# Modulation steps of the first layer, and the place of its rotations on the vector engine

## The chip, the cores and the metric

The kernel runs on one core of a Trainium2 chip, as one program. The metric is the device time of one execution in microseconds (us), the median of the runs. The core has a matrix engine (TensorE, PE), a vector engine (VectorE, DVE), a scalar engine (ScalarE, ACT), a general engine (GpSimd, POOL) and a queue that issues the transfers (SyncE, SP). Each engine works through its own instructions in its own order, and they wait for each other by semaphores.

## What is computed

The program holds a block of two layers (attention with a feed-forward part, retention with a feed-forward part) and two more hybrid layers behind it, for 256 positions of width 1024. The change touches the first layer of the first block, where half of the 16 heads are stick-breaking heads and half are block-attention heads whose q and k are rotated; with 256 positions and blocks of 256, these see only their own block, a causal softmax.

```python
def ada_mod(c, w, b):
    m = jax.nn.silu(c) @ w + b
    return jnp.split(m[:, None, :], 6, axis=-1)

def attn_hybrid_mixer(h, w_qkv, w_o, pos):
    B, S, _ = h.shape
    qkv = (h @ w_qkv).reshape(B, S, 3, N_ATT_HEADS, HEAD_DIM).transpose(2, 0, 3, 1, 4)
    q, k, v = qkv[0], qkv[1], qkv[2]
    sb = stick_breaking_attention(q[:, :N_SB_HEADS], k[:, :N_SB_HEADS], v[:, :N_SB_HEADS])
    qm = rotary(q[:, N_SB_HEADS:], pos)
    km = rotary(k[:, N_SB_HEADS:], pos)
    mb = moba_attention(qm, km, v[:, N_SB_HEADS:])
    o = jnp.concatenate([sb, mb], axis=1).transpose(0, 2, 1, 3).reshape(B, S, ATT_W)
    return o @ w_o

def first_block(...):
    for layer in range(DEPTH):
        shift_m, scale_m, gate_m, shift_f, scale_f, gate_f = ada_mod(c, ada_w[layer], ada_b[layer])
        h = modulate(rms_norm(x, norm_gains[layer, 0]), shift_m, scale_m)
        ...
        x = x + gate_m * y
        h = modulate(rms_norm(x, norm_gains[layer, 1]), shift_f, scale_f)
        x = x + gate_f * swiglu(h, ffn_w_gate_up[layer], ffn_w_down[layer])
```

## The kernel before

All products are made from pairs of rounded parts: a weight piece of 1 MB comes as `raw` (L326, SP queue), ACT casts it to `whi` (L346), DVE subtracts to get `wlo` (L347), two of each for one `raw`, and PE does three matmuls for one (L278). `raw` has three buffers in all, two for any load and one that takes every third.

The first layer's attention is in `layer0`. The projection to q, k and v of the stick-breaking heads is done in the start-up. `layer0` then makes three modulation jobs (L822; the gate, then shift and scale of the feed-forward part). `gemm_col` computes q and k of the rotated heads, two tiles of 128 rows each; as each is done, its `epi` (L850) rotates it on DVE (`rotary`, L611 to L614, from PSUM with the table `rope` into `rows`), PE transposes it (L282, `p<-ident,rows`), and ACT copies the result to `qT` or `kT` (L857). Between these matmuls stand the stick-breaking heads (`score`, `sb_job`: ACT L658 to L660 make `sbe`, DVE L661 and L663 make `sbs`, PE multiplies `sbs` by triangles, ACT L668 and DVE L669 make `aT`), their products with v (`av`, `p<-aT,v`, whose result is split into `oTq` on ACT and `oTk` on DVE, L486 and L487), then the rotated heads (`causal_job`, L627 to L637, tiles `sm` and `aT`), their products with v, and the output projection `w_ao` (`gemm_k`), behind which `res_norm` adds the residual (L549, L550) and makes the next norm (L512 to L524).

A modulation job (`ada_steps`, L559) is a matrix-vector product done on DVE. It has four steps. A step is one call of `feed` (L373): a load of 1 MB of `ada_w` into a `raw` buffer and two instructions L570, each of which adds one row block, scaled by one element of c, to `acc`. When four steps are done, `acc` is split (`acch` on ACT, L486; `accl` on DVE, L487) and two pairs of matmuls with ones sum it over the partitions into `bc` (L586, L588). Three jobs are twelve steps, 24 instructions L570. `pump` (L332) calls `feed`: for each weight load that it emits it adds `self.rate` to a credit, and one step is emitted for each whole unit of credit.

What sets the order: PE runs in program order, which a planner makes: jobs are generators that yield due times, and each matmul advances the planner's clock `now` by its modelled time. DVE, ACT, POOL and SP run in the order that the tile scheduler gives them by priority. An instruction has, in general, the priority of its place in the program; `self.first()` (L532) lifts those within it by `PRI` = 250.

Of the kernel before, what the change touches and what calls it, by code (L numbers as in the profile page):

```python
# [27 lines left out]
VLAG = 3  # L28
START = 'a0 w0 a1 a2 w1 a3 v0 a4 w2 a5 v1 a6 w3 a7'.split()
T_AO, T_DN, T_RO, T_OUT, T_O = 4, 7, 7, 8, 8  # L30
R_L0, R_FFN, R_L1 = 2.04, 0.65, 0.59
PRI = 250
D_EV0, D_ROT0, D_SOFT, D_SB = 5.11, 5.49, 11.39, 9.42
D_ADA0, D_ADAF, D_ADA1, D_FFN, D_FFN1 = 12.84, 50.82, 20.9, 11.5, 11.36
# [28 lines left out]
def chunks_of(K, blocks):  # L63
    out, off = [], 0
    kt = K // 128
    for cols in blocks:
        n, lst = len(cols), []
        step = max(1, 2048 // n)
        step = min(step, 4)
        for k0 in range(0, kt, step):  # L70
            nk = min(step, kt - k0)
            lst.append((off, k0, nk, n))
            off += 128 * nk * n
        out.append(lst)
    return out
# [169 lines left out]
class Kern:  # L245
# [569 lines left out]
    def layer0(self, lp):  # L815
        nc, V, A = self.nc, self.V, self.A
        with self.pool("l0") as p:
            self.ph, self.smb = p, 3
            hT, ps0 = self.startup(lp)
            self.tc.keep_in_program_order(A.preload_act_table_set("natural_log_exp_and_others"))  # L820
            self.rate = R_L0
            jobs = [self.ada(lp, 0, v) for v in (2, 3, 4)]  # L822
            rope = p.tile([128, 2, 3, 32], F32, name="rope64")
            nc.sync.dma_start(rope, self.a["k_rope64"].rearrange("p (t j d) -> p t j d", t=2, j=3))
            self.causal = p.tile([128, 384], F32, name="causal0")
            nc.sync.dma_start(self.causal, self.a["k_causal"])
            self.strict = p.tile([128, 2, 128], F32, name="strict")
            nc.sync.dma_start(self.strict, self.a["k_strict"].rearrange("p (j n) -> p j n", j=2))
            h = lambda k, t: (hT[t][0][:, k], hT[t][1][:, k])
            qT = [p.tile([128, 4, 256], F32, tag=f"q{j}", name=f"qT{j}") for j in range(2)]  # L830
            kT = [p.tile([128, 4, 256], F32, tag=f"k{j}", name=f"kT{j}") for j in range(2)]
            v = [p.tile([128, 2, 512], F32, tag=f"v{j}", name=f"v{j}") for j in range(2)]
            oT, aTs, sj, avj = [None, None], {}, {}, {}

            def qk0(t, w):
                rows = self.wk.tile([128, 512], F32, tag="rows", bufs=4, name=self.nm("rows"))
                A.copy(rows, ps0[t][w])
                yield D_EV0
                src = self.trs(rows, 4)
                d = (kT if w else qT)[0][:, :, t * 128:t * 128 + 128]  # L840
                if w:
                    A.copy(d, src)
                else:
                    A.activation(d, src, AF.Copy, scale=0.125)

            j0 = [self.spawn(qk0(t, w)) for t in range(2) for w in range(2)]
            for t in range(2):
                A.copy(v[0][:, t], ps0[t][2])

            def epi(b, t, _, ps):  # L850
                if b == 3:
                    A.copy(v[1][:, t], ps)
                    return
                rows = self.wk.tile([128, 512], F32, tag="rows", bufs=4, name=self.nm("rows"))
                self.rotary(rows, ps, rope, t, 8, 32)
                yield D_ROT0
                A.copy((qT if b == 1 else kT)[1][:, :, t * 128:t * 128 + 128], self.trs(rows, 4))  # L857

            def score(hd, deps):
                j, r = hd // 8, hd % 8  # L860
                pr, o = r // 2, (r % 2) * 64
                while not all(d.done for d in deps):
                    yield 0.7
                aTs[hd] = aT = p.tile([128, 3, 128], F32, tag="aT", bufs=AT0, name=self.nm("aT"))
                q, k = (lambda: qT[j][o:o + 64, pr]), (lambda: kT[j][o:o + 64, pr])
                yield from self.sb_job(q, k, aT) if j == 0 else self.causal_job(q, k, 0.125, aT)

            def av(pr, deps):
                j, r = pr // 4, pr % 4
                while not all(d.done for d in deps):  # L870
                    yield 0.7
                yield 1.5
                if oT[j] is None:
                    oT[j] = [p.tile([128, 4, 256], F32R, tag=f"{x}{j}", name=f"oT{x}{j}") for x in "qk"]
                pv = self.av_pair(v[j], 2 * r, [aTs.pop(2 * pr), aTs.pop(2 * pr + 1)])
                self.split(oT[j][0][:, r], oT[j][1][:, r], pv)

            ch = chunks_of(D, QKV_BLOCKS)
            for hd in range(8):
                sj[hd] = self.spawn(score(hd, j0), 1.0 + hd * SP_SB)  # L880
            for pr in range(4):

                avj[pr] = self.spawn(av(pr, [sj[i] for i in range(8)]), 1.0)
            qkj = self.gemm_col(h, "w_qkv", ch[1:3], epi, 1)
            for hd in range(8, 16):
                sj[hd] = self.spawn(score(hd, qkj), 0.5 + (hd - 8) * SP_MB)
            vj = self.gemm_col(h, "w_qkv", ch[3:4], epi, 3)
            for pr in range(4, 8):
                avj[pr] = self.spawn(av(pr, vj + [sj[i] for i in range(8, 16)]), 1.0)
            gate, = self.finish(jobs[0])  # L890

            def ho(k, t):
                self.wait(avj[k])
                return tuple(x[:, k % 4, t * 128:t * 128 + 128] for x in oT[k // 4])

            nxt = self.res_norm(gate, lambda: self.finish(jobs[1], jobs[2])[::-1])
            self.gemm_k(ho, "w_ao", 8, nxt.epi, tail=T_AO)
        return nxt
# [615 lines left out]
```

## Time and profile before

| | before |
|---|---|
| median of 3 runs | 1489.71 us (1488.64 to 1490.63) |
| profiled execution | 1490.03 us, span 1488.2 us |
| PE busy | 1453.1 us, 98% of the span |
| DVE busy | 1046.9 us, 70% |
| ACT busy | 814.3 us, 55% |
| mean granted clock of PE | 0.995 |

The profile is of one execution. The span runs from the first to the last instruction; the run's time has 1.8 us more around it. A line of a timeline gives the start in us, the duration, the engine, the line of the code, the operation, what it writes and reads, and, in brackets, how long the engine stood idle before it and for whom. Neighbouring rows of the same kind are put together (x16), and then the duration is that of the group. The modelled end of a matmul lies later than the start of the one behind it, so the distance of the starts is what one costs. The granted clock of PE is given as a share of its full speed.

### The profile page before, as it was taken

To read this page: it belongs to the slowest core of one execution; us is meant where nothing else is said; L and a number is where in the kernel's file an instruction comes from. 1 tells how busy PE (TensorE), PEld (TensorE's weight loads), DVE (VectorE), ACT (ScalarE), POOL (GpSimd) and SP (SyncE) were. 2 spreads that over 40 slices of the span, in tenths; PEclk is the share of its full clock that TensorE was granted. 3 is DMA by queue.
4 is the path that set the end of the run, shared out by engine and by line. 5 is a ranking of instruction groups with operands and counts; after the bars stand their busy time and mean duration, and the time that the engine had idled before them with its cause. 6 is when DMAs were issued, how large, how long until landed. Compare 5 with 4: busy or idle time off the path is not lost.

```text
span 1488.2 us, 20261 instructions
## 1 busy us (share of the span) xinstructions
PE 1453.1 (98%) x7724; PEld 1218.9 (82%) x7724; DVE 1046.9 (70%) x1677; ACT 814.3 (55%) x1369; POOL 96.8 (7%) x84
## 2 busy tenths in 40 slices
PE   7999999999999999999999999999999999999998
PEld 4776788887877888888878899988888879998887
DVE  4688898956988848866378656666666865556664
ACT  4657566643444535665266745566445664566551
POOL 0000000000000000000012011110001101111000
PEclk9999999999999999999999999999999999999999
DMA  9747587754776637745445355554645545555552
GB/s 379 275 175 278 186 327 291 285 210 180 278 277 232 257 139 266 272 170 207 150 144 198 128 183 179 178 200 166 212 140 205 170 142 188 164 173 198 184 176 79
DMA packets 52965, 306.67 MB, mean 206 GB/s; under 512 B 7546, under 2 KB 10490, under 8 KB 24580
## 3 DMA queue, kind: packets, MB, share of 16 engines
q1 hardware_dynamic: 52148, 305.14, 57.4%
q8 instruction: 61, 1.00, 0.3%
q10 hardware_dynamic: 720, 0.24, 0.1%
q14 instruction: 36, 0.29, 0.1%
HBM read 301.16 MB, written 1.05 MB: 203 GB/s over the span
## 4 chain that ended last, share of the span: by engine, by line
PE 76%; DVE 11%; ACT 4%; DMA 3%; POOL 3%; issue 2%; POOLq 0%; SPq 0%; DVEq 0%; ACTq 0%
PE p L278 73%; DVE wlo L347 5%; PE p L282 3%; DMA raw<-in_w_in_dram 3%; POOL dss L482 2%; ACT whi L346 1%; ACT dsm L1434 1%; DVE dsm L1432 1%; DVE dss L1379 1%; POOL qss L482 1%; ACT dsm L1436 1%; POOL ss L514 0%; DVE junk L522 0%; DVE rows L1381 0%; DVE res L549 0%
## 5 line engine op out<-in xcount | busy, mean ns | idle before, releaser
L278 PE MATMUL p<-whi,hT 128*128 128x512 f32 (+2 forms) x2432 | 763.7, 382 | 6.3 <-DVE hT L487 2.2
L347 DVE TENSOR_TENSOR wlo<-raw,whi 128x1024 fp32r<-128x1024 f32 (+2 forms) x474 | 538.3, 1161 | 149.3 <-ACT whi L346 146.0
L346 ACT CAST whi<-raw 128x1024 fp32r<-128x1024 f32 (+2 forms) x474 | 462.6, 1001 | 262.9 <-PE p L278 174.6
L278 PEld LDWEIGHTS p<-whi,hT 128*128 128x128 f32 x2432 | 453.1, 188 | 80.4 <-issue 8.3
L278 PE MATMUL p<-wlo,hT 128*128 128x512 f32 (+2 forms) x1216 | 453.0, 373 | 0.0
L278 PEld LDWEIGHTS p<-wlo,hT 128*128 128x128 f32 x1216 | 229.6, 189 | 30.3 <-issue 1.7
L278 PE MATMUL p<-hT,whi 128*128 128x512 f32 x576 | 199.2, 398 | 0.0
L278 PE MATMUL p<-hT,wlo 128*128 128x256 f32 x576 | 149.9, 281 | 0.0
L278 PEld LDWEIGHTS p<-hT,whi 128*128 128x128 f32 x576 | 103.8, 188 | 19.6
L278 PEld LDWEIGHTS p<-hT,wlo 128*128 128x128 f32 x576 | 108.7, 189 | 6.6
L570 DVE SCALAR_TENSOR_TENSOR acc<-raw,csc,acc 128x1024 f32<-128x1024 f32 x80 | 102.2, 1278 | 3.1 <-DMA raw<-in_ada_w_dram 2.8
L278 PE MATMUL p<-whi,al 128*128 128x512 f32 x176 | 69.5, 395 | 0.0
L278 PE MATMUL p<-wlo,ah 128*128 128x512 f32 x176 | 69.5, 395 | 0.0
L278 PE MATMUL p<-whi,ah 128*128 128x512 f32 x176 | 69.5, 395 | 0.0
L482 POOL TENSOR_TENSOR dss<-dss,mh 128x6 f32<-128x6 f32 x32 | 46.1, 1442 | 330.5 <-DVE dss L481 330.5
L1381 DVE TENSOR_TENSOR rows<-p,dss 128x384 f32<-128x384 f32 x32 | 17.8, 558 | 46.3 <-POOL dss L482 46.3
L954 ACT COPY fT<-p 128x256 f32<-128x256 f32 x72 | 25.8, 369 | 37.1 <-PE p L278 34.5
L1434 ACT ACTIVATE dsm<-dsm,dst 128x512 f32<-128x512 f32 x32 | 22.9, 716 | 41.0 <-DVE dst L1433 41.0
L514 POOL TENSOR_TENSOR ss<-ss,mh 128x1 f32<-128x1 f32 x14 | 13.4, 959 | 474.1 <-DVE ss L513 474.1
L278 PE MATMUL p<-whi,s 128*128 128x512 f32 x128 | 41.3, 397 | 0.0
L278 PEld LDWEIGHTS p<-whi,al 128*128 128x128 f32 x176 | 33.0, 187 | 8.1
L278 PEld LDWEIGHTS p<-wlo,ah 128*128 128x128 f32 x176 | 33.0, 187 | 8.0
(259 smaller groups left out, 1618.9 us busy)
## 6 DMA issues: line engine op xcount, KB each, us to landing
raw<-in_w_in_dram SPq DMA_DIRECT2D x48, 1024.0 KB, 4.9
raw<-in_w_gu_dram SPq DMA_DIRECT2D x44, 1024.0 KB, 5.6
raw<-in_ada_w_dram SPq DMA_DIRECT2D x40, 1024.0 KB, 5.0
raw<-in_w_in_dram SPq DMA_DIRECT2D x48, 768.0 KB, 4.4
raw<-in_w_ret_dram SPq DMA_DIRECT2D x24, 1024.0 KB, 4.9
raw<-in_w_dn_dram SPq DMA_DIRECT2D x22, 1024.0 KB, 5.0
raw<-in_w_qkv_dram SPq DMA_DIRECT2D x11, 1024.0 KB, 5.4
as<-in_ada_s_dram SPq DMA_DIRECT2D x16, 512.0 KB, 8.0
```

Source lines behind the costliest of these rows:

```text
L278: self.T.matmul(out, lhsT=lhsT, rhs=rhs, start=first, stop=last, skip_group_check=skip)
L282: self.T.transpose(out, in_, self.ident)
L346: for ins in (self.A.copy(hi[:, :m * n], src), self.V.tensor_tensor(lo[:, :m * n], src, hi[:, :m * n].bitcast(F32), ALU.subtract)):
L347: self.V.tensor_tensor(lo[:, :m * n], src, hi[:, :m * n].bitcast(F32), ALU.subtract)):
L482: self.G.tensor_tensor(ss, ss, self.mh[:, :n], ALU.pow)
L570: self.V.scalar_tensor_tensor(acc, r[:, j * D:j * D + D], self.sc[:, k:k + 1], acc, ALU.mult, ALU.add)
L954: A.copy(f, ps[:, 256:512])
L1379: V.tensor_reduce(ss[:, :6], sq[:, :384].rearrange("p (h d) -> p h d", d=64), AX.X, ALU.add)
L1381: V.tensor_tensor(rows[:, :384].rearrange("p (h d) -> p h d", d=64), ps.rearrange("p (h d) -> p h d", d=64), ss[:, :6, None].to_broadcast( ...
L1432: V.tensor_tensor_reduce(sm, ps[j], tabs[j][:, t * 128:t * 128 + 512], 1.0, NEG, ALU.add, ALU.max, st[:, 0:1])
L1434: A.activation(sm, sm, AF.Exp, bias=st[:, 2:3], scale=0.125, accum_out=st[:, 3:4])
L1436: A.activation(sm, sm, AF.Copy, scale=st[:, 3:4])
```

## The change

The rate at which modulation steps follow weight loads in the first layer goes from 2.04 to 1.36. Four steps, all of the first job, are emitted ahead of the loads of the three small tables (`rope`, `causal`, `strict`). And the rotation in `epi` stands within `self.first()`. In the changed file lines behind L822 are two lines further down, and those behind the rotation three.

```diff
-R_L0, R_FFN, R_L1 = 2.04, 0.65, 0.59
+R_L0, R_FFN, R_L1 = 1.36, 0.65, 0.59
...
             jobs = [self.ada(lp, 0, v) for v in (2, 3, 4)]
+            for _ in range(4):
+                self.feed()
             rope = p.tile([128, 2, 3, 32], F32, name="rope64")
...
                 rows = self.wk.tile([128, 512], F32, tag="rows", bufs=4, name=self.nm("rows"))
-                self.rotary(rows, ps, rope, t, 8, 32)
+                with self.first():
+                    self.rotary(rows, ps, rope, t, 8, 32)
                 yield D_ROT0
```

How this orders the engines, at three places. First DVE, where the first rotated tile (`rows_739` before, `rows_759` after) is made, directly behind the weight subtractions of the fourth projection load. Before:

```order
L611 TENSOR_TENSOR rows_739<-p_646,rope_624 128x512
L612 TENSOR_TENSOR rt_740<-p_646,rope_624 128x8x32
L613 TENSOR_TENSOR rt_740<-p_646,rope_624 128x8x32
L614 TENSOR_TENSOR rows_739<-rows_739,rt_740 128x512
L570 SCALAR_TENSOR_TENSOR acc_779<-raw_783,csc,acc_779 128x1024
L661 SCALAR_TENSOR_TENSOR sbs_700<-p_696,sbe_699 128x384
L570 SCALAR_TENSOR_TENSOR acc_779<-raw_783,csc,acc_779 128x1024
```

And after, the same place on DVE, where `acc_624` is the first job's sum:

```order
L570 SCALAR_TENSOR_TENSOR acc_624<-raw_632,csc,acc_624 128x1024 x2
L661 SCALAR_TENSOR_TENSOR sbs_720<-p_716,sbe_719 128x384
L570 SCALAR_TENSOR_TENSOR acc_624<-raw_636,csc,acc_624 128x1024
L661 SCALAR_TENSOR_TENSOR sbs_731<-p_727,sbe_730 128x384
L570 SCALAR_TENSOR_TENSOR acc_624<-raw_636,csc,acc_624 128x1024
L661 SCALAR_TENSOR_TENSOR sbs_742<-p_738,sbe_741 128x384
L570 SCALAR_TENSOR_TENSOR acc_624<-raw_640,csc,acc_624 128x1024
L611 TENSOR_TENSOR rows_759<-p_666,rope_644 128x512
L612 TENSOR_TENSOR rt_760<-p_666,rope_644 128x8x32
L613 TENSOR_TENSOR rt_760<-p_666,rope_644 128x8x32
L570 SCALAR_TENSOR_TENSOR acc_624<-raw_640,csc,acc_624 128x1024
L614 TENSOR_TENSOR rows_759<-rows_759,rt_760 128x512
```

The rotation's four instructions now stand behind the first job's steps and three L661, and within the last step; before, they stood ahead of all of these.

On ACT, the copy of that tile's transposes to `qT`. Before:

```order
L660 ACTIVATE sbe_759<-sbe_759 128x384
L659 ACTIVATE sbe_801<-sbe_801 128x384
L857 COPY qT_631<-p_811 128x4x128
L660 ACTIVATE sbe_801<-sbe_801 128x384
L668 ACTIVATE aT_695<-p_696 128x384
```

And after, on ACT at the same place (`acch_799` is the high part of the first job's sum, `raw_789` the next projection load):

```order
L660 ACTIVATE sbe_821<-sbe_821 128x384
L486 CAST acch_799<-acc_624 128x1024
L346 CAST whi_791<-raw_789 128x1024
L346 CAST whi_795<-raw_789 128x1024
L860 COPY qT_651<-p_831 128x4x128
L668 ACTIVATE aT_715<-p_716 128x384
```

The copy now stands behind the split of the first job's sum and behind two weight casts.

The third place is the second half of the output projection, on ACT, with the four casts `oTq` of the rotated heads' results (`raw_1335` and `raw_1421` before are the first two loads of the feed-forward part's weights, `raw_1343` and `raw_1391` after). Before:

```order
L486 CAST acch_1358<-acc_1205 128x1024
L486 CAST oTq_1382<-p_1384 128x256
L346 CAST whi_1337<-raw_1335 128x1024
L346 CAST whi_1341<-raw_1335 128x1024
L486 CAST oTq_1382<-p_1391 128x256
L486 CAST oTq_1382<-p_1398 128x256
L486 CAST oTq_1382<-p_1405 128x256
L346 CAST whi_1423<-raw_1421 128x1024
L346 CAST whi_1427<-raw_1421 128x1024
```

And after, on ACT:

```order
L346 CAST whi_1345<-raw_1343 128x1024
L346 CAST whi_1349<-raw_1343 128x1024
L486 CAST acch_1353<-acc_1024 128x1024
L637 COPY aT_1256<-p_1380 128x384
L346 CAST whi_1393<-raw_1391 128x1024
L346 CAST whi_1397<-raw_1391 128x1024
L486 CAST oTq_1401<-p_1403 128x256
L486 CAST oTq_1401<-p_1413 128x256
L486 CAST oTq_1401<-p_1420 128x256
```

All four `oTq` now stand behind the casts of the second load of the feed-forward part, whose first cast moved ahead of them from behind them. On DVE `oTk` moved in the same way behind `wlo_1394` and `wlo_1398`, and on PE three matmuls of the projection now follow the first product with v, where before all four products came first.

## Rows read from the trace of the kernel before

**Rows 1.** The page's part 4: the chain that ended last, by engine.

```profile
PE 76%; DVE 11%; ACT 4%; DMA 3%; POOL 3%; issue 2%; POOLq 0%; SPq 0%; DVEq 0%; ACTq 0%
```

**Rows 2.** Stretches of 20 us: busy us (instructions) by engine, clock, DMA share, GB/s.

```profile
80.00:100.00 20.00, 16.46 (x85) 13.77 (x85) 19.43 (x31) 11.60 (x23) 0.07 (x1) 0.92 0.58 219
...
180.00:200.00 20.00, 20.00 (x102) 16.91 (x101) 17.28 (x21) 11.07 (x18) 0.00 (x0) 1.00 0.85 317
```

**Rows 3.** The same view for short stretches; the clock is the third number from the end.

```profile
97.00:98.00 1.00, 0.13 (x1) 0.16 (x2) 1.00 (x4) 0.84 (x1) 0.00 (x0) 0.50 0.98 393
98.00:103.00 5.00, 5.00 (x14) 4.06 (x15) 3.28 (x8) 0.79 (x2) 0.95 (x1) 0.50 0.88 338
103.00:104.00 1.00, 1.00 (x7) 0.89 (x6) 0.64 (x1) 0.00 (x0) 0.00 (x0) 0.72 0.07 29
...
165.00:171.00 6.00, 4.54 (x24) 3.29 (x23) 6.00 (x11) 4.30 (x8) 0.79 (x1) 1.00 0.00 0
```

**Rows 4.** Timeline of PE, from 94 us: the second rotated tile's transposes.

```profile
97.87 1.09 PE L282 MATMUL p<-ident,rows 128*128 128x128 f32 x4 [3.38 <-DVE rows L614]
```

**Rows 5.** Timeline of PE, 80 to 83 us: the first rotated tile's transposes.

```profile
80.57 0.60 PE L282 MATMUL p<-ident,rows 128*128 128x128 f32 x4
...
82.03 0.92 PE L278 MATMUL p<-qT,kT 64*128 64x256 f32 x4 [0.16 <-ACT qT L857]
```

**Rows 6.** Timeline of DVE: first rotation, L661 and L570, start of the second rotation.

```profile
69.92 0.69 DVE L611 TENSOR_TENSOR rows<-p,rope 128x512 f32<-128x512 f32 x1 [3.58 <-PE p L282]
...
74.42 0.56 DVE L661 SCALAR_TENSOR_TENSOR sbs<-p,sbe 128x384 f32<-128x384 f32 x1 [1.22 <-ACT sbe L660]
74.89 1.28 DVE L570 SCALAR_TENSOR_TENSOR acc<-raw,csc,acc 128x1024 f32<-128x1024 f32 x1
76.08 0.42 DVE L663 TENSOR_TENSOR sbs<-sbs,strict 128x256 f32<-128x256 f32 x1
...
82.68 0.68 DVE L611 TENSOR_TENSOR rows<-p,rope 128x512 f32<-128x512 f32 x1
```

**Rows 7.** DVE, 60 to 200 us, by shape: busy us, mean ns, idle before.

```profile
L347 DVE TENSOR_TENSOR wlo<-raw,whi 128x1024 fp32r<-128x1024 f32 x33 | 39.2, 1218 | 3.6 <-ACT whi L346 3.6
...
L611 DVE TENSOR_TENSOR rows<-p,rope 128x512 f32<-128x512 f32 x4 | 2.7, 687 | 5.3 <-PE p L282 3.6 <-PE p L278 1.7
...
L612 DVE TENSOR_TENSOR rt<-p,rope 128x256 f32<-128x256 f32 x4 | 1.7, 416 | 0.0
```

**Rows 8.** ACT, 60 to 200 us, by shape.

```profile
L346 ACT CAST whi<-raw 128x1024 fp32r<-128x1024 f32 x32 | 32.8, 1050 | 9.4 <-DMA raw<-in_w_gu_dram 5.0 <-PE p L278 3.1 <-DMA raw<-in_w_ao_dram 1.1
...
L857 ACT COPY qT<-p 128x512 f32<-128x512 f32 x2 | 1.2, 585 | 0.8 <-PE p L282 0.8
```

**Rows 9.** Timeline of the SP queue, 60 to 67 us.

```profile
60.49 0.33 SPq L326 DMA_DIRECT2D raw<-in_w_qkv_dram  x1
...
63.84 2.85 SPq L326 DMA_DIRECT2D raw<-in_ada_w_dram  x2
```

**Rows 10.** The page's part 6: loads of modulation weights, KB each, median us to landing.

```profile
raw<-in_ada_w_dram SPq DMA_DIRECT2D x40, 1024.0 KB, 5.0
```

**Rows 11.** PE's waits, 60 to 180 us: total us, times, longest.

```profile
PE p L278 <- ACT aT L637: 1.0, 2, 0.6
PE p L282 <- ACT sm L635: 0.9, 2, 0.7
```

**Rows 12.** Timeline of ACT, 150 to 154 us.

```profile
150.08 0.37 ACT L486 CAST oTq<-p 128x256 fp32r<-128x256 f32 x1 [0.43 <-PE p L278]
...
153.48 2.01 ACT L346 CAST whi<-raw 128x1024 fp32r<-128x1024 f32 x2 [0.32 <-DMA raw<-in_w_gu_dram]
```

**Rows 13.** Timeline of PE, 149 to 152 us: products with v of the rotated heads.

```profile
149.16 2.82 PE L278 MATMUL p<-aT,v 128*64 128x256 f32 x32
```

**Rows 14.** Timelines of DVE and PE at the layer's end, 160 to 167 us.

```profile
160.53 1.28 DVE L550 TENSOR_TENSOR x<-x,res 128x512 f32<-128x512 f32 x2
...
166.24 1.03 PE L282 MATMUL p<-ident,junk 128*128 128x128 f32 x8
```

## The prediction

> **What bounds the kernel now.** I read the page's chain first: three quarters of it is TensorE (PE), so an edit on other engines moves the time only where PE waits for them, or where PE's clock changes [rows 1]. The table of 20 us stretches then says where that can be: from 180 us on PE is busy for all of every stretch, also where modulation steps run beside it, and between 80 and 100 us it is busy for only 16.46 us [rows 2]. The change acts between 60 and 180 us; behind that it only shuffles steps in stages without PE waits, and I put nothing on them.
>
> The largest PE wait there is 3.38 us before 97.87: the four transposes of the second rotated tile wait for the last addition of its rotation (L614) [rows 4]. On VectorE (DVE) the tile's first multiplication (L611) had started at 82.68 [rows 6]; its other three instructions follow much later, between modulation steps (L570) of 1.28 us. The one-microsecond windows show a second loss behind the wait: the granted clock is 0.50 from 97 to 103 and 0.72 in the next microsecond, that is 1.2 GHz in place of 2.4 [rows 3]. It cost 0.50 x 0.13 + 0.50 x 5.00 + 0.28 x 1.00 = 2.84 us of PE time. Short waits that add up to 1.46 us within 165 to 171 us left it at 1.00 [rows 3]. So wait and slow clock together are worth some 6.4 us, and this is what the change can win: 3.6 us of start delay (I add 0.2 us to each wait shown, since a matmul's modelled end lies later than the start that its successor has without a wait) and 2.84.
>
> **The change part by part.** No instruction's work is added or removed: the twelve steps with their 24 L570 are there before and after in the first layer. The steps move, the loads of the three tables move behind four of them, and the rotations move on DVE.
>
> *The lower rate and the priority, at the second rotation.* After the change its four instructions stand together, behind the first job's last split and with one weight subtraction between. They end some 5.5 us after the first rotation, at about 88, and PE wants them at about 94.5. Cover: 6 us. So the wait of 3.6 us and, with it, the 2.84 us of half clock go. Only the later waits decide if that is kept.
>
> *The first rotation, on DVE.* Before, its four instructions ran at 69.92 while DVE had nothing else, and PE found them ready at 80.57 without a wait [rows 5]. Now the first job's steps stand ahead: all of the third load's and half of the fourth's, alternating with three L661. The first L661 is bound by ScalarE (ACT) and starts at 74.42 as now [rows 6]. From there: three L661 at 0.47 apart, three L570 at 1.19 apart [rows 6], then L611 0.60, L612 and L613 0.33 each, one more L570 1.19, and L614 0.69 like L611 in full (the others are the means of their groups less the 0.09 us by which neighbours overlap) [rows 7]. 74.42 + 1.41 + 3.57 + 0.60 + 0.66 + 1.19 + 0.69 = 82.54. PE arrives at 80.57 [rows 5] and waits about 2.05 us. If the first L661 started later, this would grow one for one; if the loads come late, too. Nothing ahead of PE's arrival changes, so I see no way under 1.5; above, 4.
>
> *The same place, on ACT.* PE does the transposes (0.35) and three matmuls (0.7), and at about 83.7 wants a score matmul whose bank the copy of the rotated tile frees: before, that copy ran at once and PE waited 0.16 [rows 5]. Now the split of the modulation row, which waits for the last L570 (81.85), and two weight casts stand ahead of the copy: 81.95 + 3 x 0.96 + 0.58 = 85.4, with the split taken as long as a cast of the same shape [rows 8]. PE waits 1.75 in place of some 0.3. Range: 0 if PE comes that much later, 2.2 if the casts' load is late.
>
> *The moved loads, on the SP queue.* The queue issues in order. The rope table was issued ahead of all modulation loads. Now four of 1 MB each stand ahead of it. Buffers come free at 60.49, 63.84 and about 66.4 (the loads issued behind the tables now; the third is the second of the pair, at its end) [rows 9], and the fourth only when the first load has landed (5.0 us [rows 10]) and two L570 have used it, about 68.8. So the table is issued near 69.2; if it takes as long as a load of 1 MB, it is there by 75. Its first user is at 79.4: cover 4 us, cost nothing. The two masks are issued right behind it, and their first users come later still.
>
> *The second half of the heads.* Four small waits of PE come from softmax and copies (1.0 and 0.9 us shown, 2.7 with the 0.2 each) [rows 11]. With the new order two L570 in a row (2.38) stand on DVE ahead of the fourth head's row maximum. They replace idle DVE time in part. I take one wait of 2.5 in place of the four, net 0 (between -2.7 and +0.6).
>
> *The output projection's second half.* Before, PE did four products of probabilities and v in a row (149.16, 2.82 us) [rows 13], and the first matmul on their result came behind the fourth; ACT's casts oTq had started at 150.08, one of them ahead of two weight casts [rows 12]. Now PE has three such matmuls directly behind the first product, ACT has two casts of the second gate-up load ahead of all four oTq, and DVE has those two subtractions ahead of all four oTk. The casts wait for the load: in the trace it lets them start at 153.48 [rows 12]. If they start then, the second ends at 155.5, its subtraction (1.22 [rows 7]) at 156.7, oTk at 157.1, where PE wanted it at 149.9 + 0.46: a wait of 6.8. If the load is long there, what is left is the cast and the subtraction of the product itself, about 0.9. PE however reaches this place 2.5 us later by the wait above, which does not hold the load back: 6.8 - 2.5 = 4.3. I take 4.0, range 0.9 to 6.8.
>
> *The end of the layer.* The first norm's chain on DVE has no slack: L550 at 160.53, and PE's transposes follow at 166.24 directly behind its last matmul [rows 14]. Now two bc instructions (0.6 each) come ahead of x's second half, and a weight subtraction (1.13) ahead of ss. That is 0 to 2.3; part of it lies beside ACT's sum of squares, so I take 1.4.
>
> *PE's clock.* Row first: one wait of 3.38 brought the clock down [rows 3, 4], short ones of 1.46 in sum did not [rows 3]. The pair of 2.05 and 1.75 with 1.05 us of work between and the 4.0 us of the projection (in two parts, 0.46 of work between) lie nearer to the first. I take 1.0 us for the pair (half of the slow time is spent waiting for ACT anyway) and 2.2 for the projection, each 0 to 2.84. The Trainium skill (TensorE: Matmul & The Clock Gate, HAM oscillation) says that a wait of PE that crosses the gate's window makes the work behind it run cold; by that alone the single long gap counts, the pair with work in it would not, and the sum would be 1.0 us lower. This case's one fall, behind 3.38 us of waiting, agrees with it, and no run here shows a broken pair yet.
>
> **Sum.** -3.6 (second rotation) - 2.84 (its slow clock) + 2.05 + 1.75 - 0.3 (first rotation) + 0 + 4.0 + 1.4 + 1.0 + 2.2 = +5.7 us. The profiled run took 1490.03 us (its span is 1488.2), 0.3 us above the median of the runs, so I forecast 1490.03 + 5.7 - 0.3 = 1495.4.
>
> **Rivals.**
>
> *Faster, about 1483.5.* The removed wait and its clock (6.4 us) are kept, because the work put ahead of the first rotation is covered: this needs the four L570 to be done by 72 us, that is all four loads in by then. For it: DVE stands idle 3.58 us before 69.92. Against it: the fourth load gets its buffer only at 68.8. It decides at a first rotation ending by 80.5 and a projection wait under 1 us; then 1490 - 6.4 + 0 to 1 = 1483.5 to 1485.
>
> *Same, about 1491.* The new waits come as summed but break up into pieces that leave the clock at 2.4 GHz: the sum without its 3.2 us of clock is +2.5, and with a projection wait of 2.5 in place of 4.0 it is +1.0, so 1490.7 to 1492.2. For it: no single new wait is as long as the 3.38 that brought the clock down, but for the projection's.
>
> *More falls, about 1499.* Also the wait at the fourth head (2.5) and the layer's end bring the clock down, 2 us each: 1499 to 1500.
>
> *It doesn't do what it says.* The rotation has priority but its table and banks are late, so DVE, in order, holds everything behind L611. With the table 4 us later than worked out, the first rotation's wait grows by 1 to 3: 1497.
>
> **How the numbers follow.** Two runs of this kernel can be told apart from about 0.2% (3 us): same is 1486.7 to 1492.7. Forecast, slower with one or two falls, 1493 to 1498: 0.52. More falls 0.10. Priority without effect 0.06. Waits without falls 0.22. Faster 0.10. So faster 0.10, same 0.22, slower 0.68. The range 1489.5 to 1500 leaves out the faster case, a little of the same one and the top of the falls: two in ten.
>
> **What would show it.** In the trace after: the second rotation's transposes without a wait, and the clock at 1.00 behind them; the first rotation's transposes with 2 us of wait on L614, and the score matmul behind them with 1.5 to 2 on the copy of the rotated tile; the first matmul on the second oTq with 2 to 4 us on ACT, then on DVE oTk; the granted clock at 0.50 for several us behind one or both. Wrong would be: the first rotation ready when PE comes (then faster), no window below 0.9 from 60 to 180 us (then same), or a PE wait behind 200 us that isn't there now.

## The result and the profile after

The changed kernel took 1501.59 us (median of four runs, 1497.32 to 1502.69), the kernel before 1489.72 (1488.64 to 1490.63): a ratio of 1.0071, with a 95% interval of 1.0058 to 1.0084. It is slower, as forecast, but by 11.9 us where 5.7 were summed, and 1501.59 lies above the range's end of 1500.

The profiled execution of the kernel after took 1497.32 us (span 1495.4, mean clock 0.992); it is the quickest of the four. The other three had mean clocks of 0.988 to 0.991. The profiled execution before had 0.995. The two totals on the page already say where to look; first the page's part 1 (busy time of each engine, its share of the span, instructions) and the chain by engine, which answers to [rows 1]:

```profile
PE 1456.9 (97%) x7724; PEld 1221.2 (82%) x7724; DVE 1047.4 (70%) x1677; ACT 816.7 (55%) x1369; POOL 98.1 (7%) x84
...
PE 80%; DVE 9%; ACT 3%; DMA 3%; POOL 2%; issue 2%; POOLq 0%; SPq 0%; DVEq 0%; ACTq 0%
```

PE was busy for 1453.1 of 1488.2 us before and for 1456.9 of 1495.4 now, with the same 7724 matmuls. So of the 7.2 us by which the span grew, 3.4 are PE idle time (38.5 us in place of 35.1), and 3.8 are the same matmuls taking longer. The second part is the clock, as the windows further down show.

**The waits.** PE's waits between 60 and 190 us in the kernel after (total us, times, longest), which answer to [rows 4, 5, 11 to 14]:

```profile
PE p L278 <- ACT oTq L486: 3.4, 1, 3.4
PE p L282 <- ACT sm L635: 1.9, 1, 1.9
PE p L282 <- DVE rows L614: 1.9, 1, 1.9
PE p L278 <- DVE hT L487: 1.5, 1, 1.5
PE p L282 <- DVE junk L524: 1.1, 1, 1.1
PE p L278 <- ACT qT L860: 0.9, 1, 0.9
PE p L278 <- DVE oTk L487: 0.8, 1, 0.8
```

The 3.38 us of [rows 4] are gone. Each line of the new list stands at a place that the prediction named: the first rotation (rows, qT), the fourth head's softmax (sm), the projection's second half (oTq, oTk) and the layer's end (junk, hT). The first five of these places in PE's timeline (start, length, instruction, then the idle time before it and its releaser):

```profile
82.45 0.69 PE L282 MATMUL p<-ident,rows 128*128 128x128 f32 x4 [1.86 <-DVE rows L614]
...
85.30 1.64 PE L278 MATMUL p<-qT,kT 64*128 64x256 f32 x4 [0.88 <-ACT qT L860]
...
134.41 1.09 PE L282 MATMUL p<-ident,sm 128*128 128x128 f32 x3 [1.86 <-ACT sm L635]
...
153.85 0.50 PE L278 MATMUL p<-whi,oTq 128*128 128x512 f32 x1 [3.37 <-ACT oTq L486]
...
155.36 0.79 PE L278 MATMUL p<-whi,oTk 128*128 128x512 f32 x1 [0.78 <-DVE oTk L487]
```

**What holds PE up.** The first rotation in the timeline of DVE: the multiplication L611 stands between two modulation steps, and the last addition L614 behind the second of them. On ACT the copy of the rotated tile (L857 before, L860 now) follows the split and two casts, and the four oTq follow a pair of casts that waits for a load:

```profile
78.06 1.28 DVE L570 SCALAR_TENSOR_TENSOR acc<-raw,csc,acc 128x1024 f32<-128x1024 f32 x1
79.25 0.68 DVE L611 TENSOR_TENSOR rows<-p,rope 128x512 f32<-128x512 f32 x1
...
80.52 1.27 DVE L570 SCALAR_TENSOR_TENSOR acc<-raw,csc,acc 128x1024 f32<-128x1024 f32 x1
81.71 0.68 DVE L614 TENSOR_TENSOR rows<-rows,rt 128x512 f32<-128x512 f32 x1
```

```profile
82.78 1.99 ACT L346 CAST whi<-raw 128x1024 fp32r<-128x1024 f32 x2
84.67 0.57 ACT L860 COPY qT<-p 128x512 f32<-128x512 f32 x1
...
151.53 1.99 ACT L346 CAST whi<-raw 128x1024 fp32r<-128x1024 f32 x2 [0.57 <-DMA raw<-in_w_gu_dram]
153.43 0.36 ACT L486 CAST oTq<-p 128x256 fp32r<-128x256 f32 x1
```

**The clock.** [rows 3] had one fall behind 60 us. After, there are three. These are short stretches (busy us and instructions of PE, PEld, DVE, ACT and POOL, then granted clock, DMA share, GB/s):

```profile
82.00:83.00 1.00, 0.55 (x5) 0.56 (x6) 1.00 (x4) 1.00 (x2) 0.00 (x0) 0.97 0.79 98
83.00:89.00 6.00, 5.12 (x15) 3.71 (x15) 4.56 (x9) 2.27 (x4) 0.95 (x1) 0.50 0.66 246
89.00:90.00 1.00, 1.00 (x5) 0.82 (x5) 0.54 (x1) 0.47 (x1) 0.00 (x0) 0.62 0.01 4
134.00:135.00 1.00, 0.59 (x2) 0.38 (x3) 1.00 (x2) 1.00 (x4) 0.00 (x0) 0.57 0.20 82
135.00:137.00 2.00, 2.00 (x7) 1.61 (x6) 2.00 (x8) 2.00 (x8) 0.00 (x0) 0.50 0.28 57
137.00:138.00 1.00, 1.00 (x5) 0.82 (x4) 1.00 (x1) 1.00 (x3) 0.00 (x0) 0.72 0.91 360
154.00:155.00 1.00, 0.58 (x2) 0.14 (x2) 1.00 (x2) 0.00 (x0) 0.00 (x0) 0.81 1.01 426
155.00:161.00 6.00, 5.64 (x27) 3.65 (x28) 1.51 (x4) 1.12 (x3) 0.00 (x0) 0.50 0.54 193
161.00:162.00 1.00, 1.00 (x5) 0.77 (x5) 0.07 (x1) 0.00 (x0) 0.00 (x0) 0.78 0.00 0
```

In each line, the clock that was missing (1 less the clock) times PE's busy time is what the fall cost: 2.96 us behind the first rotation, 1.53 behind the fourth head, 3.15 behind the projection, 7.64 in sum against 2.84 before. This is an upper price: for the 4.8 us more, PE's busy time over the whole span grew by 3.8. The lines also tell when each fall began. At the rotation the clock was still up for nearly all of the stretch from 82 to 83, so it fell some 0.5 us behind the first wait and ahead of the second (0.88, from 84.4); at the fourth head it fell at about 134.1, inside the wait, which had then lasted 1.6 us. A matmul of 512 columns takes 0.63 us in these stretches and 0.40 outside them.

### The profile page after: what moved, and what is told of

The parts are those of the page before. It is cut to its first block, busy times and chain, and to the rows that moved or that the text cites. A ratio compares the mean times of both kernels' runs of the same rounds, so it can differ in the third digit from the quotient of the medians.

```text
span 1495.4 us, 20247 instructions
## 1 busy us (share of the span) xinstructions
PE 1456.9 (97%) x7724; PEld 1221.2 (82%) x7724; DVE 1047.4 (70%) x1677; ACT 816.7 (55%) x1369; POOL 98.1 (7%) x84
## 4 chain that ended last, share of the span: by engine, by line
PE 80%; DVE 9%; ACT 3%; DMA 3%; POOL 2%; issue 2%; POOLq 0%; SPq 0%; DVEq 0%; ACTq 0%
PE p L278 77%; DVE wlo L347 4%; PE p L282 4%; DMA raw<-in_w_in_dram 2%; POOL dss L482 1%; ACT whi L346 1%; ACT dsm L1437 1%; POOL qss L482 1%; DVE dsm L1435 1%; POOL ss L514 0%; DVE dss L1382 0%; ACT dsm L1439 0%; DVE junk L522 0%; DVE acc L570 0%; DMA raw<-in_w_gu_dram 0%
## 5 line engine op out<-in xcount | busy, mean ns | idle before, releaser
L570 DVE SCALAR_TENSOR_TENSOR acc<-raw,csc,acc 128x1024 f32<-128x1024 f32 x80 | 102.2, 1277 | 11.7 <-DMA raw<-in_ada_w_dram 11.5
```

Of the source, the lines that this page charges most:

```text
L570: self.V.scalar_tensor_tensor(acc, r[:, j * D:j * D + D], self.sc[:, k:k + 1], acc, ALU.mult, ALU.add)
```

## The experiments

Every kernel ran beside the kernel before on the same chip, whose medians were 1490.85, 1490.91 and 1490.97 us in the three groups (e1 to e4, e5 to e8, e9 to e12). The first theory is the prediction's, with one thing added after the first result: the waits came as summed and are small, and the rest is PE's clock, which falls behind them at more places and in more executions than the prediction counted. The rivals were that the waits vary from run to run, or that the stages behind 180 us lost time that one trace does not show.

**e1: the kernel after again.** No edit.

> The changed kernel unaltered, again, to see what differs between its executions (1497.32 to 1502.69 us so far, where before spans 2 us) and whether the trace that was read is a typical one. Theory (clock): the same PE waits as in the first trace within 0.3 us, but falls of PE's clock of other lengths or at other waits; times spread over 3 us or more, and the runs with the lower mean clock are the longer ones, about 1.5 us for each 0.001 of mean clock. Rival (a transfer): the falls are the same, and one PE wait is longer by 1 us or more, since a load landed later.

Measured: 1501.23 us, ratio 1.0069 (1.0046 to 1.0092). The six executions line up by their mean clock:

| us | 1495.52 | 1499.18 | 1499.92 | 1502.55 | 1504.79 | 1506.17 |
|---|---|---|---|---|---|---|
| clock | 0.993 | 0.990 | 0.989 | 0.988 | 0.986 | 0.986 |

The slope is 10.65 us for 0.007, some 1.5 us for each 0.001, which is what 0.001 of a 1500 us span would be if the slow stretches are nearly all busy. The one in the middle was profiled. Its waits are those of the first trace but for the one on qT (1.50 us in place of 0.88), and its falls are others. In PE's timeline and in the windows, behind the waits at the rotation, the fourth head, and much later in the second half of the program:

```profile
84.23 0.65 PE L282 MATMUL p<-ident,rows 128*128 128x128 f32 x4 [1.85 <-DVE rows L614]
...
137.16 0.84 PE L282 MATMUL p<-ident,sm 128*128 128x128 f32 x3 [1.87 <-ACT sm L635]
```

```profile
86.00:93.00 7.00, 5.92 (x18) 5.06 (x19) 4.40 (x9) 2.05 (x5) 0.95 (x1) 0.55 0.44 184
137.00:141.00 4.00, 3.76 (x11) 2.90 (x12) 4.00 (x9) 4.00 (x13) 0.00 (x0) 0.61 0.44 156
158.00:161.00 3.00, 2.28 (x11) 1.47 (x13) 0.67 (x2) 0.00 (x0) 0.00 (x0) 0.56 0.62 197
1135.00:1137.00 2.00, 2.00 (x11) 1.97 (x10) 1.85 (x3) 0.99 (x2) 0.00 (x0) 0.50 0.60 178
```

The fall at the projection is half as long as in the first trace, behind the same waits (3.64 and 0.78), and there is one at 1135 us behind a wait of PE on the junk of a norm (2.40). The kernel before has that wait too, and no fall behind it. Its timeline and a window around it:

```profile
1124.92 1.23 PE L282 MATMUL p<-ident,junk 128*128 128x128 f32 x8 [2.47 <-DVE junk L522]
```

```profile
1120.00:1140.00 20.00, 17.53 (x90) 15.37 (x89) 13.54 (x25) 11.60 (x30) 1.54 (x3) 1.00 0.49 170
```

So the same wait may bring the clock down in one execution and not in another, and one trace cannot give the number of falls that stands behind a median.

Not all of e1's slow time lies where the change acts. There is a fall near 766 us too, and the fall in the start-up, which every trace has and which the change does not touch, is longer than in the kernel before. The core of both falls in e1, and of the start-up's in the kernel before:

```profile
15.00:25.00 10.00, 8.91 (x32) 5.01 (x32) 3.63 (x10) 2.00 (x7) 0.00 (x0) 0.50 1.02 417
...
766.00:769.00 3.00, 2.83 (x8) 2.71 (x9) 2.56 (x5) 0.37 (x2) 1.40 (x1) 0.50 0.03 6
```

```profile
15.00:21.00 6.00, 5.42 (x22) 2.34 (x22) 2.27 (x4) 0.19 (x1) 0.00 (x0) 0.50 1.02 415
```

Priced like the others, e1's falls cost 8.4 us more than those of the kernel before: 3.6 between 60 and 180 us, 3.2 at 766 and 1135 us, and 1.7 in the start-up. Its span grew by 9.8 us, of which 3.0 are PE idle time (38.1 us) and 6.8 are PE's busy time (1459.9).

**e2: the kernel after, with matmuls that change nothing in PE's new gaps.** A matrix of zeros is multiplied ahead of the transposes (into a bank that they overwrite) and between the projection's matmuls (adding zero): eight at the first rotation, eight at the fourth head, 13 and 3 at the projection. The order of the rest stays, but for what makes the zeros.

```
+    def fill(self, ps, n, add=False):
+        for _ in range(n):
+            self.T.matmul(ps, lhsT=self.zero_r, rhs=self.H[:, 0, 0, 0:4], start=not add, stop=not add, ...)
...
-                self.trs(rows, 4))
+                self.trs(rows, 4, fill=8 if b == 1 and t == 0 else 0))
```

> The changed kernel with PE kept busy in three of its new waits: 8 matmuls of a zero matrix ahead of the first rotated tile's transposes, 8 ahead of the fourth rotated head's, 13 and 3 that add zero ahead of the two waits for oTq and oTk. At 0.23 us each that is 1.84, 1.84, 2.99 and 0.69 us, about the waits themselves (1.86, 1.86, 3.37, 0.78). Nothing else on any engine is in another order but for the making of the zero matrix at the start. Theory (clock): the granted clock stays at 1.00 from 60 to 180 us, and the time falls by the 7.6 us that the three falls of the first trace cost, to about 1490, with a spread near 2 us. Rival (the waits are the whole loss): within 1.5 us of the changed kernel run beside it, or above it.

Measured: 1493.51 us (1491.31 to 1499.74, twelve runs), ratio 1.0019 (1.0007 to 1.0032). Work that computes nothing made the kernel 7.7 us faster. In the profiled execution the clock does not fall between 60 and 180 us:

```profile
60.00:180.00 120.00, 114.70 (x587) 88.33 (x586) 101.01 (x171) 77.13 (x158) 4.88 (x5) 1.00 0.63 230
```

The data that PE waits for do not come earlier (L614 of the first rotation ends at 84.7 us, in e1 at 84.2), so this gain is the clock's; the median of the runs' mean clocks rose from e1's 0.9885 to 0.993. The time was 3.5 us more than expected and the spread wider; the trace shows falls further on that were left alone, of 1.55 us at 756 us and 1.47 at 1125 us.

**e3 and e4: the parts.** e3 is the kernel before with the priority alone; e4 is the kernel before with the four early steps and the lower rate, without the priority.

```
+                with self.first():
-                self.rotary(rows, ps, rope, t, 8, 32)
+                    self.rotary(rows, ps, rope, t, 8, 32)
```

> Before with the rotation in self.first() and nothing else: no early steps, rate 2.04. Theory (the early steps cause the first rotation's wait, the priority removes the second's): PE finds the first rotated tile ready at 80.6, and the second one too, so 3.4 us of wait and 2.84 us of clock go in that stretch; later waits come from DVE's new order, above all at the last job's sum, whose steps now end late. In sum between 1488 and 1497. Rival (the priority alone is the harm): the wait at the first rotation is there also here.

Measured: 1499.0 us, ratio 1.0049 (1.0034 to 1.0064), 2 us above the range expected. Both rotations are ready when PE comes, so the priority does what it says. But twelve steps that give way at the rotations must end by the same place, and now the last of them are late. PE's timeline shows the sum over a modulation row, which the layer's end needs, waiting for its split (in this execution, the quickest of four, the wait itself is most of the loss: PE was idle for 40.6 us in place of 35.1 and busy for 1454.6 in place of 1453.1):

```profile
165.53 0.80 PE L278 MATMUL p<-acch,ones_r 128*128 128x512 f32 x1 [9.13 <-ACT acch L486]
```

> The change without the priority: four early steps and rate 1.36, the rotation as before. Theory (the early steps are what delays the first rotation): its transposes wait for L614 for 4 to 5 us, more than the 1.86 with priority, and the second rotation's wait for 1 us or none; time 1497 to 1503. Rival (the priority is the harm): the first rotation is ready when PE comes, and the time is near 1490.

Measured: 1502.55 us, ratio 1.0079 (1.0063 to 1.0095). Without the priority the first rotation holds PE up for 3.99 us in place of 1.86:

```profile
84.55 1.11 PE L282 MATMUL p<-ident,rows 128*128 128x128 f32 x4 [3.99 <-DVE rows L614]
```

**e5: the projection's wait taken away at its cause.** In the kernel after, the splits of the rotated heads' results get priority over the weight casts and subtractions.

```
-                self.split(oT[j][0][:, r], oT[j][1][:, r], pv)
+                with self.first():
+                    self.split(oT[j][0][:, r], oT[j][1][:, r], pv)
```

> The changed kernel, with the casts oTq and subtractions oTk of the heads' results in self.first() too, so that ACT and DVE do them ahead of the weight casts of the second gate-up load. Theory (the projection's wait comes from these casts): the waits of 3.4 and 0.8 us for oTq and oTk shrink to 1.2 or less each, and the fall of the clock behind them goes or gets shorter; 3 us less for the waits and 0 to 3 for the clock, so 1494 to 1498.5 where the changed kernel takes 1501. Rival (the load is late, the casts only stand behind it): the waits stay above 3 us, time as the changed kernel within 1.5 us.

Measured: 1494.68 us (1489.41 to 1497.65, twelve runs), ratio 1.0022 (1.0008 to 1.0035), 6.9 us under the kernel after's first median and 6.6 under e1's. The other waits are unchanged (1.86, 1.91, 1.11 and 1.49); those of the projection have shrunk to what the product's own cast and subtraction take, and no fall follows them in the profiled execution:

```profile
149.30 0.50 PE L278 MATMUL p<-whi,oTq 128*128 128x512 f32 x1 [0.50 <-ACT oTq L486]
...
150.62 0.49 PE L278 MATMUL p<-whi,oTk 128*128 128x512 f32 x1 [0.59 <-DVE oTk L487]
```

The wait that left is 3.4 + 0.8 - 1.1 = 3.1 us. The rest, 3.5 to 4 us, fits the clock: the median of the runs' mean clocks is 0.992, where the kernel after had 0.990 and e1 0.9885. In this execution the fourth head's wait of 1.91 brought no fall either (a window around it):

```profile
130.00:140.00 10.00, 8.02 (x39) 6.03 (x39) 9.97 (x33) 8.95 (x29) 0.00 (x0) 1.00 0.49 156
```

**e6: both, and fills further on.** e5 with fills at the rotation and the fourth head (8 each), fewer at the projection (5 and 3), and matmuls with the unit matrix ahead of three norms' transposes: one at the first norm behind the attention and at the first norm of the hybrid layers, two at the second of these.

```
+        for _ in range(x):
+            self.T.matmul(pt, lhsT=self.ident, rhs=self.x[0][:, 0:512], start=True, stop=True, ...)
...
-            src = self.trs(xn[:, n * 512:n * 512 + 512], 4)
+            src = self.trs(xn[:, n * 512:n * 512 + 512], 4, x={(1, 0): 1, (7, 0): 1, (9, 0): 2}.get((self.norms, n), 0))
```

> The kernel with the split in self.first(), and PE kept busy with matmuls that change nothing in its remaining waits (8 at the first rotation, 8 at the fourth head, 5 and 3 at the projection, one of four passes at the first norm behind the attention and at the first hybrid layer's norm, two at the second's). Theory (clock): no stretch at half clock behind 30 us, so it is below before: 1483 to 1487, spread under 4 us. Rival (PE's clock falls by something else than these waits): half-clock stretches stay, time 1489 or more.

Measured: 1486.33 us (1483.62 to 1491.45, nine runs), ratio 0.9973 (0.9959 to 0.9986). It is the only kernel that beats both. In the profiled execution (1487.07 us, clock 0.996) the clock stays up from the start-up to the end:

```profile
30.00:1480.00 1450.00, 1436.68 (x7657) 1211.53 (x7656) 1033.46 (x1641) 803.81 (x1348) 95.20 (x77) 1.00 0.57 204
```

The spread of 7.8 us is wider than expected, so some executions still have falls. And this does not show that the change is good: the fills at the later norms may help the kernel before as well, which was not tried.

**e7 and e8: the order of the steps.** e7 is the kernel after with the old rate of 2.04; e8 has the four early steps behind the loads of the three tables.

> The change without the lower rate: four early steps and priority, rate 2.04. Theory (the early steps alone make the first rotation's two waits; the lower rate, by which the last job ends later, makes the projection's): first rotation 1.9 and 0.9 to 1.5 as in the changed kernel, no wait over 1 us for oTq; a new wait of 2 us near 108 where steps crowd; the fourth head's wait stays near 1.9. Time 1493 to 1499, 2 to 6 below the changed kernel. Rival (the lower rate has no part in the projection's wait): the wait for oTq is 3 us or more.

Measured: 1498.75 us, ratio 1.0047 (1.0032 to 1.0063). The oTq wait is gone, the first rotation's (1.85) stays, and a wait of 2.08 on DVE comes at a head in between:

```profile
117.84 1.11 PE L278 MATMUL p<-aT,v 128*64 128x256 f32 x8 [2.08 <-DVE aT L669]
```

> The change with the four early steps emitted behind the three tables' loads instead of ahead of them. On DVE the first rotation then stands ahead of all but one L570, and the L661 and L663 of the heads stand behind. Theory (DVE has too much work in 70 to 83 us, whatever stands first): no wait for the first rotation, but one of 1.5 to 2.5 us shortly after, for sbs; time within 3 us of the changed kernel. Rival (the tables' late loads or the rotation's place is the cause): the wait in 78 to 84 us goes, and nothing of over 1 us takes its place before 100 us; 4 us or more are won.

Measured: 1497.09 us (1492.87 to 1501.17), ratio 1.0037 (1.0021 to 1.0052). The first rotation no longer waits, but the scores behind it do, and so does oTk:

```profile
86.26 1.14 PE L278 MATMUL p<-sbs,sq 128*128 128x256 f32 x6 [1.67 <-DVE sbs L663]
...
154.34 0.70 PE L278 MATMUL p<-whi,oTk 128*128 128x512 f32 x1 [2.65 <-DVE oTk L487]
```

It is 4 us under the kernel after, more than the theory's 3 and as much as the rival asked for; but the rival also wanted no wait of over 1 us in the old one's place, and the 1.67 stands there. In both the waits move along DVE rather than vanish.

**e9 and e10: the price of the falls, place by place.** e9 is the kernel after with only the eight fills ahead of the first rotation, e10 with only the 13 and 3 at the projection.

> The changed kernel with PE kept busy only ahead of the first rotated tile's transposes (8 matmuls of a zero matrix, 1.84 us). It measures the clock term of that place, which the prediction put at 1.0 us. Theory (each fall costs what the trace shows, 3.0 us of slow work at this place): 2 to 3.5 us below the changed kernel, 1498 to 1499.5; the falls at the fourth head and the projection stay. Rival (half of it is waited for anyway, as predicted): 0.5 to 1.5 us below.

Measured: 1497.36 us, ratio 1.0040 (1.0027 to 1.0053), 3.9 under the median of e1. The prediction had put 1.0 on the clock there. The fall at the rotation shrank but did not go: PE's wait on the copy qT, 1.4 us, still stands behind the fills. By its trace the fall cost 1.7 us in place of 3.0 to 3.2, so no more than 1.5 of the 3.9 us are seen at this place.

```profile
86.00:89.00 3.00, 3.00 (x12) 2.52 (x11) 2.21 (x3) 0.49 (x1) 0.00 (x0) 0.59 0.50 182
```

> The changed kernel with PE kept busy only in the projection's two waits (13 and 3 matmuls that add zero, 2.99 and 0.69 us). It measures the clock term of that place, which the prediction put at 2.2 us. Theory: 2 to 3.5 us below the changed kernel, 1498 to 1499.5; the falls at the first rotation and the fourth head stay. Rival (the falls are tied to each other, so that one that goes brings another): within 1 us of the changed kernel.

Measured: 1494.23 us, ratio 1.0014 (1.0001 to 1.0028), 7.0 under e1, where 2.2 had been put on the clock and 2 to 3.5 were expected. In its trace nothing falls from 143 us to the layer's end, while the two falls ahead stay:

```profile
85.00:95.00 10.00, 9.05 (x29) 7.29 (x29) 7.49 (x15) 5.05 (x8) 0.95 (x1) 0.51 0.42 158
139.00:143.00 4.00, 3.93 (x13) 3.04 (x13) 3.60 (x9) 4.00 (x12) 0.00 (x0) 0.59 0.61 195
143.00:180.00 37.00, 33.54 (x169) 25.30 (x168) 27.16 (x42) 20.33 (x41) 1.62 (x3) 1.00 0.49 178
```

The two gains add up to 10.9, more than e2's 7.7, which has both. The kernel after was not run again in this group; it is held against e1, whose ratio alone has an interval of 3.4 us to each side, so each gain holds to some 4 us, not better. The 7.0 at the projection is above the predicted 2.2 even so; whether it is more than the 3.15 that the first trace's fall cost stays open. The 3.9 at the rotation does not show by itself that more than the predicted 1.0 was lost there; the traces' 2.96 and 3.21 do.

**e11 and e12: the two remaining parts apart.** e11 is the kernel before with the rate of 1.36 alone, e12 the kernel before with the four early steps alone.

> Before with the rate 1.36 and nothing else. By order, no step stands ahead of the first rotation, and the last job's steps are done late. Theory (a part that moves steps later makes a wait at the end of the layer): the first rotation without a wait, one of 1 us or less at the second, and a wait of several us, up to 10, of the last job's sum (acch); 1494 to 1500. Rival (the lower rate only thins the steps out on DVE): no wait over 2 us behind 100 us, and the time is at most that of before.

Measured: 1498.23 us, ratio 1.0046 (1.0031 to 1.0061). Both rotations are ready, and the sum at the layer's end is late by 9.58 us, as in e3:

```profile
161.85 0.79 PE L278 MATMUL p<-acch,ones_r 128*128 128x512 f32 x1 [9.58 <-ACT acch L486]
```

> Before with the four early steps ahead of the tables and nothing else, rate 2.04. Theory (the early steps delay the first rotation, and without priority more): its transposes wait 3.5 to 4.5 us, further waits of 2 to 5 us at the second half of the heads; 1499 to 1506, above the changed kernel or near it. Rival (early steps free DVE later, as intended): first rotation under 2 us, time below 1495.

Measured: 1500.99 us, ratio 1.0062 (1.0042 to 1.0082), with waits of 4.00 at the first rotation and 4.38 at the fourth head:

```profile
145.16 1.09 PE L282 MATMUL p<-ident,sm 128*128 128x128 f32 x3 [4.38 <-ACT sm L635]
```

So no part alone, and neither of the pairs tried (e4, e7), beats the kernel before. The early steps are needed if the rest are to be spread or to give way, and they cost the first rotation its cover.

## Why the prediction was right in direction and too small

**Right: where the waits go and come.** Sizes as shown in the first trace of after, with 0.2 added to a wait where the prediction did so:

| term | predicted | measured |
|---|---|---|
| second rotation's wait | -3.6 | -3.6: L614 done at 87.5, no wait |
| its slow clock | -2.84 | gone: the falls now stand elsewhere |
| first rotation | +2.05 | 1.86 shown, 2.06 |
| qT behind the casts | +1.75, less 0.3 of before | 0.88 in the first trace, 1.50 in e1, less 0.3 |
| tables behind four loads | 0, issued at 69.2 | 0, issued at 69.12 |
| fourth head | one wait of 2.5 for four, net 0 | one wait of 1.86 for four (1.9), net 0 |
| output projection | +4.0 | 3.37 and 0.78, so 4.15 |
| layer's end | +1.4 | 1.1 and 1.5 for 0.75 and 0.72, so 1.1 |
| clock, rotation | +1.0 | 2.96 in the first trace, 3.21 in e1 |
| clock, projection | +2.2 | 3.15 in the first trace, 1.48 in e1 |
| clock, fourth head | 0 (a rival of 0.10) | 1.53 in the first trace, 1.70 in e1 |
| clock, behind 180 us | 0 | 0 in the first trace, 3.2 in e1 |

The waits' terms sum to +5.3 by the prediction and to some +4.3 by the table (with the first trace's 0.88); the page's idle time grew by 3.4. The projection's size came out by luck: the two casts ahead of oTq started at 151.53, not 153.48, and PE wanted the result at 150.48, not 2.5 us later than before (152.9); both are some 2 us early, and the wait between them came out near the sum. The queue of the table loads is one line of the SP queue's timeline, and the second rotation's end one of DVE's:

```profile
69.12 0.43 SPq L826 DMA_DIRECT2D rope<-in_k_rope_dram  x1
```

```profile
86.86 0.68 DVE L614 TENSOR_TENSOR rows<-rows,rt 128x512 f32<-128x512 f32 x1
```

**The step that failed: "PE's clock".** Four things in it were wrong. It put 1.0 us on the pair of waits at the first rotation, on the ground that half of the slow time would be spent waiting; PE was busy for 5.12 of the 6 slow us, and the fall cost 2.96. (Some of that did come off the second wait: 0.88 us, where e1, whose clock fell at that wait's end, has 1.50.) It left the fourth head at nothing, because a single wait of about 2 us was shorter than the 3.38 that it knew; 1.86 was enough, in both traces. It put nothing on the time behind 180 us, as stages in which PE does not wait, and showed one window for it (180 to 200 us); the kernel before has waits there, of 2.47 us at 1124.92 for one, with PE busy for 17.53 of 20 us, and at these places e1 lost 3.2 us. And it took the one fall of one execution of the kernel before as what a fall is: the sum then has a fixed number of falls, while the executions have different ones. With the profiled runs the clock's share is 3.8 us where the prediction has +3.2 - 2.84 = +0.4. In the medians the mean clock went from 0.995 to 0.990 in the first four runs and to 0.9885 in e1, which at e1's 1.5 us for 0.001 is 7.5 of 11.9 us and 9.8 of 10.4. PE's busy time, the other measure, grew by 6.8 us in e1's trace. So the waits were, if anything, summed too high, and the clock cost some 7 to 10 us in the median in place of 0.4: that is the gap between the forecast and the result. How much of the clock's part the kernel before also loses in some of its executions, in the start-up and behind 180 us, its one trace does not tell.

By the rule that the prediction quoted (the Trainium skill, TensorE: Matmul & The Clock Gate, HAM oscillation) the pair of waits with work in it would leave the clock alone. The trace does not agree: 0.50 from 83 to 89, and the clock had fallen behind the first wait of 1.86 alone, before the second began. The same page's section "A second HAM failure mode: psum-queue depth-cycling" tells of another kernel, in which short idles of PE between groups of matmuls were frequent enough to make the clock swing as well. No run here shows that case: PE was busy for 4.54 of the 4.55 us ahead of the fourth head's wait, and the fall there stands at that one wait.

**The rivals.** More falls (1499, 0.10) came nearest: the fall at the fourth head came, the one at the layer's end did not in either trace, falls behind 700 us came that it had not named, and its price was still too low. Same (0.22) rested on no wait being as long as 3.38 but the projection's; the falls at 1.86 refute it. The faster case needed the four steps to be done by 72 us; the last of them started at 80.52. The priority is not without effect: e4 shows 3.99 where after has 1.86.

**What stays open.** Why a wait brings the clock down in one execution and not in the next isn't settled. At the norm near 1125 us, a wait of 2.47 left it up in before and one of 2.6 in the first trace of after, while 2.40 in e1 and 2.60 in e2 brought it down; at the fourth head 1.86 brought it down in the first trace of after and 1.91 in e5 did not. The kernel before seems to have such executions too: its times beside the experiments run from 1487.97 to 1495.92 us, and 11 of these 63 executions have a mean clock of 0.993 or less. The experiments show that filling the gap keeps it up in most executions, and what a lower mean clock costs; they do not show what decides at the edge.

## What to carry to other kernels

Where one engine is busy for 97% of the span, a new short wait of that engine is to be priced with the clock it may cost: here waits of 1.9 to 3.6 us each brought a loss of 1.5 to 3.2 us, not in every execution, and the median held the sum. Read the mean clock of all runs beside their times before trusting one trace; if times line up by it, the question is not which instruction is slow but which gaps there are. And steps that are only moved (earlier, later, behind a priority) keep their total on the engine: ask what each is then ahead of, for every place it could stand, and if gaps must be, cheap matmuls that change nothing can be worth as much as a better order (e2: 7.7 us, e5: 6.6), though neither alone brought this kernel back to the time before.

## What the runs showed of the hardware that was not expected

At a wait of 1.86 us, with PE busy before and after it, the clock fell to 1.2 GHz (0.50) in both traces of after, in one of them before the wait was over, while 2.47 us in the kernel before left it up. The same program's time ran from 1495.5 to 1506.2 us in step with its mean clock, 0.993 to 0.986. And PE doing nothing useful was faster than PE waiting: with fills the stretch from 60 to 180 us went from a mean clock of 0.93 to 1.00.
